# Products of the layer borders and the gated product of the classical FFN tiles kept in PSUM instead of SBUF

## The chip, the cores and the metric

The kernel runs on one core of one Trainium2 chip. The metric is the device time of one execution in microseconds (us), as the median of several executions. Six resources matter here: TensorE (PE, with its weight loads PEld), VectorE (DVE), ScalarE (ACT), GpSimd (POOL), and the DMA queue that SyncE (SP) issues to. TensorE writes its results to PSUM, which has banks of 512 float32 per partition; DVE and ACT read and write PSUM and SBUF, POOL works on SBUF alone.

## What is computed

Two layers of a trunk over 512 latent and 256 context tokens, width 1024. A layer is a half-step SwiGLU FFN, a token mixer (a gated DeltaNet group beside latent attention), and a second half-step FFN. Every sub-layer is wrapped in the same way:

```python
def pre_mod(x, g, m, slot):
    return rmsnorm(x, g) * (1 + m[:, None, 3 * slot + 1]) + m[:, None, 3 * slot]

def post_residual(x, y, g, m, slot, weight):
    return x + weight * m[:, None, 3 * slot + 2] * rmsnorm(y, g)

def ffn_sublayer(x, m, slot, g_pre, g_post, wg, wu, wd):
    h = pre_mod(x, g_pre, m, slot)
    y = (jax.nn.silu(h @ wg) * (h @ wu)) @ wd
    return post_residual(x, y, g_post, m, slot, 0.5)
```

So between any two sub-layers there is a *border*: the sum of squares of y, its norm's factor, the residual, the sum of squares of the new x, that norm's factor, and the modulated input of the next sub-layer.

## The kernel before

**Layout.** Activations lie transposed: eight tiles of 128 features, each with 768 token columns. Columns are worked on in three groups of 256: G_A and G_B (latent) and G_C (context). In what follows a letter behind a stage names its group (z_A, post_B). Every matrix product is made of three float32r products, from a high and a low part of both operands, so each border ends by splitting its result z into `zh` (rounded) and `zl` (the rest).

**The border** is a generator per group. `post` (L414) waits for the sum of squares `ss` of y; `rb1` (L145) reduces it on PE into a PSUM bank of two buffers (`aux`, L137), DVE and POOL make the factors (L158, L159), and `rb2` (L162) has PE broadcast them over all partitions, into columns 0 to 255 of the same bank (R). ACT copies R into SBUF (L425). For each of the eight feature tiles a product y*R goes to a slot `t` (L432: on DVE for five tiles, on POOL for tiles 0, 3 and 5), and DVE adds t times the gate to x (L434). ACT squares the new x, and POOL and DVE in turn add the squares up (L404, L405). `prez` (L448) makes the factors of the next norm by `rb1` and `rb2`, and `z_tile` (L465) works per feature tile: DVE multiplies x, a column and R (read from PSUM) into a slot t (L469), ACT adds the shift and rounds, which gives zh (L472). Towards an FFN (slot 0 or 2), ACT also writes the unrounded z into y (L476), and zl is z minus zh (L477: DVE for even tiles, POOL for odd). Towards the mixer (slot 1) even tiles make zl on DVE straight from t (L479), and odd tiles by ACT in place and POOL (L481, L482).

The slots of `post` and `z_tile` are the same ring: `slot(1)` (L391) hands out three pieces of 256 columns of one SBUF tile in turn, whoever asks.

**The FFN.** Its first three column tiles of hidden features (f = 0, 1, 2) are computed "classically", by `mm3` from zh and zl: f = 0 and 1 group by group while the border still runs, f = 2 afterwards over all columns. `evac` (L541) turns the two banks of a tile, gate `pg` and up `pu`, into the hidden value in pieces of 256 columns: ACT Silu of pg into SBUF `sg` (L546), DVE product of pu and sg into sg (L547), ACT rounds sg into `gh` (L538), DVE writes the rest into `gl` (L539). Banks for matrix products come from a ring of six (`bank`, L131). All other tiles (f = 3 to 21) go by `fast`, a Strassen-like scheme whose operands `combine` (L550) prepares on DVE, ACT and POOL from y right after the border (L560 to L578); its own evacuation (L616 to L619) already keeps the product in its bank.

**What sets the order.** Borders run beside matrix work: `down` (L753) and `mix_out` produce y group by group and call `step()` between products, which advances the generators of the groups before; `mix_pre` (L826) does the same while the next products of the mixer run, and `ffn` while tiles f = 0 and 1 do. `drain(g)` runs a group's generator to its end. This is the program order. Each engine's own queue is then written by the framework's scheduler (`schedule_with_timeline_sim=True`), which goes through the program in order of priority and time; work under `high_priority` comes first. On the chip each queue runs strictly in that order, and an instruction that waits holds up those behind it. Adaptive-norm vectors of later stages are computed by DVE in the background (`pump`, `flush`, L243).

Of the kernel before, what the change touches and what calls it, by code (L numbers as in the profile page):

```python
# [20 lines left out]
EPS = 1e-6  # L21
# [13 lines left out]
class K:  # L35
# [126 lines left out]
    def rb2(self, ps, r, n):  # L162

        for t in range(n // P):
            self.nc.tensor.matmul(ps[:, t * P : (t + 1) * P], r[:, t : t + 1].to_broadcast([P, P]), self.ident, start=True, stop=True)
        return ps[:, :n]

    def rbcast(self, ss, n, inv_d, eps):
        return self.rb2(*self.rb1(ss, n, inv_d, eps))
# [75 lines left out]
    def begin(self):  # L245
# [17 lines left out]

        def factor(g):
            r = self.new_rs()
            nc.scalar.copy(r, self.rbcast(xs[g], g[1], 1.0 / 1024, EPS))
            return r

        m = {part: self.cp.tile([P, KT, 2], F32, name=f"m0_0_{part}") for part in range(2)}
# [35 lines left out]
        for q in range(4):  # L305
# [32 lines left out]
                R = {g: factor(g) for g in (G_A, G_B)}  # L338
            for g in (G_A, G_B):
                for k in (2 * q, 2 * q + 1):  # L340
                    self.z_tile(0, 0, g, R[g], k)
            yield
        load_x(G_C)

# [70 lines left out]
    def post(self, l, slot, g, ss, final=False, nxt=None):  # L415

        nc = self.nc
        off, n, v = g
        for _ in range(1):
            yield  # L420
        rb = self.rb1(ss, n, 1.0 / 1024, EPS)
        for _ in range(1):
            yield
        R = self.new_rs()
        nc.scalar.copy(R, self.rb2(*rb))  # L425
        pg = self.pg[l, slot]
        ss2 = None if final else self.ssx
        first = [True, True]
        for k in range(KT):
            t = self.slot(1)  # L430
            eng = nc.gpsimd if (41 >> k) & 1 else nc.vector
            eng.tensor_tensor(out=t, in0=self.y[k][:, off : off + n], in1=R, op=ALU.mult)  # L432
            xs = self.X[k][:, off : off + n]
            nc.vector.scalar_tensor_tensor(out=xs, in0=t, scalar=pg[:, k, v : v + 1], in1=xs, op0=ALU.mult, op1=ALU.add)  # L434
            if final:
                nc.sync.dma_start(self.out[:, k, off : off + n], xs)
            else:
                i = (178 >> k) & 1
                self.sumsq(ss2[i], xs, first[i], nc.vector if i else nc.gpsimd)
                first[i] = False  # L440
            if k % 3 == 2:
                yield
        if not final:
            for _ in range(3):
                yield
            yield from self.prez(nxt[0], nxt[1], g, ss2)

    def prez(self, l, slot, g, ss):  # L448
        nc = self.nc
        off, n, v = g  # L450
        yield
        rb = self.rb1(ss, n, 1.0 / 1024, EPS)
        for _ in range(1):
            yield
        R = self.rb2(*rb)
        for k in range(KT):
            self.z_tile(l, slot, g, R, k)
        if slot != 1 and (l, slot) != (0, 0):

            if (l, slot) not in self.xsv:  # L460
                self.xsv[l, slot] = self.dram_tile(f"xs{l}{slot}", [KT, P, NT])
            for k in range(KT):
                nc.sync.dma_start(self.xsv[l, slot][k][:, off : off + n], self.X[k][:, off : off + n])

    def z_tile(self, l, slot, g, R, k):  # L465
        nc = self.nc
        off, n, v = g
        t = self.slot(1)
        nc.vector.scalar_tensor_tensor(out=t, in0=self.X[k][:, off : off + n], scalar=self.scol[l, slot][:, k, v : v + 1], in1=R, op0=ALU.mult, op1=ALU.mult)  # L469
        h, lo = self.zh[k][:, off : off + n], self.zl[k][:, off : off + n]  # L470
        b = self.M[l, slot, 0][:, k, v : v + 1]
        nc.scalar.activation(h, t, AF.Identity, bias=b)  # L472
        if slot != 1:

            zf = self.y[k][:, off : off + n]
            nc.scalar.activation(zf, t, AF.Identity, bias=b)  # L476
            (nc.vector if (85 >> k) & 1 else nc.gpsimd).tensor_sub(lo, zf, h.bitcast(F32))  # L477
        elif (85 >> k) & 1:
            nc.vector.scalar_tensor_tensor(out=lo, in0=t, scalar=b, in1=h.bitcast(F32), op0=ALU.add, op1=ALU.subtract)  # L479
        else:  # L480
            nc.scalar.activation(t, t, AF.Identity, bias=b)  # L481
            nc.gpsimd.tensor_sub(lo, t, h.bitcast(F32))  # L482

    def open_w(self):
        self.wp = self.pool("w", side="right")
# [38 lines left out]
    def ffn(self, l, i, slot, groups, post, begin=None):  # L524
# [7 lines left out]
        def loads(f, eng=None):  # L532
            return [self.load_w(d["wu"][l, i, f, u], eng=eng) for u in range(2)]

        def gated(j, h, off, n):
            with self.hp(0):
                o = gh[j][:, off : off + n]
                nc.scalar.copy(o, h)  # L538
                nc.vector.tensor_sub(gl[j][:, off : off + n], h, o.bitcast(F32))  # L539

        def evac(j, pg, pu, off, n):  # L541
            for o in range(0, n, 256):
                sg = self.sg()[:, :256]
                c = slice(o, o + 256)
                with self.tc.high_priority():
                    nc.scalar.activation(sg, pg[:, c], AF.Silu)  # L546
                    nc.vector.tensor_tensor(out=sg, in0=pu[:, c], in1=sg, op=ALU.mult)  # L547
                gated(j, sg, off + o, 256)

        def combine():  # L550

# [282 lines left out]
    def mix_in(self, l, last):  # L834
# [127 lines left out]
        def low_rank(t0, cnt, gain, dst, groups, inv_d):  # L962
# [28 lines left out]
            def scaled():  # L991
              for g in gs:
                off, n, v = g
                R = self.rb2(*rb[g])
                for j in range(cnt):
                    x = st[j][:, off : off + n]
                    nc.vector.scalar_tensor_tensor(out=x, in0=x, scalar=gain[:, j : j + 1], in1=R, op0=ALU.mult, op1=ALU.mult)
# [1018 lines left out]
```

## Time and profile before

| | us |
|---|---|
| median of 3 executions | 3329.84 |
| lowest, highest | 3324.64, 3330.06 |
| the profiled execution's own time | 3321.82 |
| its span, first to last instruction | 3320.0 |
| PE busy | 3058.4 (92%) |
| DVE busy | 2562.9 (77%) |
| ACT busy | 1377.4 (41%) |
| POOL busy | 1345.7 (41%) |

The profile is one execution, recorded by the hardware. Busy is time in which an instruction of the engine ran; an "idle before" is the time an engine sat still before an instruction, with the instruction (engine, tile, line) that ended the wait behind an arrow. A group's mean is over all instructions of one line, engine and operand shape. `ps`, `mixp` and `rb` are PSUM tiles, `bt` the slots, `be` sums of squares and R, `m` the modulation columns.

### The profile page before, as it was taken

To read this page: it belongs to the slowest core of one execution; us is meant where nothing else is said; L and a number is where in the kernel's file an instruction comes from. 1 tells how busy PE (TensorE), PEld (TensorE's weight loads), DVE (VectorE), ACT (ScalarE), POOL (GpSimd) and SP (SyncE) were. 2 spreads that over 40 slices of the span, in tenths; PEclk is the share of its full clock that TensorE was granted. 3 is DMA by queue.
4 is the path that set the end of the run, shared out by engine and by line. 5 is a ranking of instruction groups with operands and counts; after the bars stand their busy time and mean duration, and the time that the engine had idled before them with its cause. 6 is when DMAs were issued, how large, how long until landed. Compare 5 with 4: busy or idle time off the path is not lost. (4 is left out here: it accounts for less than half of the span.)

```text
span 3320.0 us, 53695 instructions
## 1 busy us (share of the span) xinstructions
PE 3058.4 (92%) x20836; PEld 2785.7 (84%) x20836; DVE 2562.9 (77%) x4337; ACT 1377.4 (41%) x2600; POOL 1345.7 (41%) x1060
## 2 busy tenths in 40 slices
PE   7899999889889998999998899999989788989998
PEld 4799989878787798999998798999877676788998
DVE  7888887777778959677777977777677879776777
ACT  4333223544445644322234432223454346544343
POOL 5322122544655765222215511221544546753233
PEclk8999999889999899999999999999989899989999
DMA  6233333222310122323324233332322310224233
GB/s 221 101 122 122 107 127 117 94 73 54 97 64 10 51 86 81 108 91 107 101 73 158 82 109 114 121 127 89 104 98 64 88 46 17 91 90 134 96 106 98
DMA packets 149816, 318.68 MB, mean 96 GB/s; under 512 B 38185, under 2 KB 79529, under 8 KB 149561
## 3 DMA queue, kind: packets, MB, share of 16 engines
q1 hardware_dynamic: 149560, 315.25, 28.9%
q8 instruction: 163, 2.67, 0.3%
q14 instruction: 93, 0.75, 0.1%
HBM read 285.17 MB, written 30.03 MB: 95 GB/s over the span
## 5 line engine op out<-in xcount | busy, mean ns | idle before, releaser
L94 POOL TENSOR_TENSOR wlo<-wraw,whi 128x1024 fp32r<-128x1024 f32 (+1 forms) x228 | 580.3, 2554 | 1357.5 <-ACT whi L93 1304.9
L93 ACT CAST whi<-wraw 128x1024 fp32r<-128x1024 f32 (+2 forms) x482 | 469.5, 978 | 692.0 <-PE ps L776 338.5
L519 PE MATMUL ps<-zh,whi 128*128 128x256 f32 (+1 forms) x1208 | 389.5, 331 | 25.2 <-DVE sg L547 13.3
L608 PE MATMUL ps<-zh,whi 128*128 128x384 f32 (+1 forms) x1216 | 392.2, 323 | 8.0 <-DVE sg L547 4.5
L609 PE MATMUL ps<-zl,whi 128*128 128x384 f32 (+1 forms) x1216 | 392.1, 322 | 2.5 <-DVE zl L586 2.5
L610 PE MATMUL ps<-zh,wlo 128*128 128x384 f32 (+1 forms) x1216 | 390.8, 322 | 0.0
L520 PE MATMUL ps<-zl,whi 128*128 128x256 f32 (+1 forms) x1208 | 382.9, 327 | 5.0 <-DVE zl L477 5.0
L775 PE MATMUL ps<-gh,whi 128*128 128x512 f32 (+1 forms) x1008 | 349.5, 354 | 21.3 <-ACT gh L618 18.9
L776 PE MATMUL ps<-gl,whi 128*128 128x512 f32 (+1 forms) x1008 | 338.3, 352 | 17.3 <-DVE gl L619 17.3
L522 PE MATMUL ps<-zh,wlo 128*128 128x256 f32 (+1 forms) x1208 | 351.1, 324 | 0.0
L94 DVE TENSOR_TENSOR wlo<-wraw,whi 128x1024 fp32r<-128x1024 f32 (+1 forms) x254 | 298.1, 1175 | 31.3 <-ACT whi L93 29.9
L778 PE MATMUL ps<-gh,wlo 128*128 128x512 f32 (+1 forms) x1008 | 293.3, 348 | 0.0
L519 PEld LDWEIGHTS ps<-zh,whi 128*128 128x128 f32 x1208 | 236.8, 199 | 56.8 <-DVE sg L547 14.0
L520 PEld LDWEIGHTS ps<-zl,whi 128*128 128x128 f32 x1208 | 238.3, 198 | 24.5 <-DVE zl L477 6.1
L775 PEld LDWEIGHTS ps<-gh,whi 128*128 128x128 f32 x1008 | 191.7, 192 | 65.2 <-ACT gh L618 21.8
L608 PEld LDWEIGHTS ps<-zh,whi 128*128 128x128 f32 x1216 | 229.4, 189 | 10.9 <-ACT whi L93 4.8
L243 DVE CUSTOM_DVE_ANT_0 abraw<-abraw,srow 128x1024 f32<-128x1024 f32 x128 | 208.0, 1625 | 33.2 <-DMA abraw<-in_wat 31.2
L776 PEld LDWEIGHTS ps<-gl,whi 128*128 128x128 f32 x1008 | 193.5, 192 | 46.7 <-DVE gl L619 19.6
L609 PEld LDWEIGHTS ps<-zl,whi 128*128 128x128 f32 x1216 | 229.5, 189 | 3.5 <-DVE zl L586 3.2
L610 PEld LDWEIGHTS ps<-zh,wlo 128*128 128x128 f32 x1216 | 229.4, 189 | 0.0
L522 PEld LDWEIGHTS ps<-zh,wlo 128*128 128x128 f32 x1208 | 222.4, 199 | 6.5 <-issue 1.0
L243 DVE CUSTOM_DVE_ANT_0 adot<-abraw,srow 128x1024 bf16<-128x1024 f32 x96 | 151.3, 1576 | 63.2 <-DMA abraw<-in_wat 62.8
(394 smaller groups left out, 7722.3 us busy)
## 6 DMA issues: line engine op xcount, KB each, us to landing
wraw<-in_wu SPq DMA_DIRECT2D x176, 512.0 KB, 3.3
abraw<-in_wat SPq DMA_DIRECT2D x128, 512.0 KB, 3.3
wraw<-in_wd SPq DMA_DIRECT2D x88, 512.0 KB, 3.5
wraw<-in_wi SPq DMA_DIRECT2D x44, 512.0 KB, 3.4
wraw<-in_wo SPq DMA_DIRECT2D x16, 512.0 KB, 4.0
xs<-x SPq DMA_DIRECT2D x64, 128.0 KB, 1.7
x<-xs SPq DMA_DIRECT2D x64, 128.0 KB, 3.4
x<-in_x SPq DMA_DIRECT2D x48, 128.0 KB, 3.7
```

Source lines behind the costliest of these rows:

```text
L93: nc.scalar.copy(hi[:, :n], raw[:, :n])
L94: (eng or nc.gpsimd).tensor_sub(lo[:, :n], raw[:, :n], hi[:, :n].bitcast(F32))
L243: self.nc.vector.tensor_tensor_reduce(out=dst, in0=w, in1=self.srow[:, v, a:b], scale=1.0, scalar=start, op0=ALU.mult, op1=ALU.add, accum_ ...
L519: nc.tensor.matmul(ps, wh, self.zh[k][:, off : off + n], start=first, stop=False)
L520: nc.tensor.matmul(ps, wh, self.zl[k][:, off : off + n], start=False, stop=False)
L522: nc.tensor.matmul(ps, wl, self.zh[k][:, off : off + n], start=False, stop=last)
L608: nc.tensor.matmul(ps, w[0][:, c], xh, start=k == 0, stop=False)
L609: nc.tensor.matmul(ps, w[0][:, c], xl, start=False, stop=False)
L610: nc.tensor.matmul(ps, w[1][:, c], xh, start=False, stop=k == 3)
L775: nc.tensor.matmul(ps, wh[:, o : o + P], gh[j][:, off : off + n], start=j == 0, stop=False)
L776: nc.tensor.matmul(ps, wh[:, o : o + P], gl[j][:, off : off + n], start=False, stop=False)
L778: nc.tensor.matmul(ps, wl[:, o : o + P], gh[j][:, off : off + n], start=False, stop=j == nf - 1)
```

## The change

Four edits, all in PSUM banks that are there already.

- `rb2` returns the whole bank. `post` reads R where it stands, without ACT's copy, and puts its products into columns 256 and on of that bank. All eight products run on DVE.
- `z_tile` puts t of even tiles into that half of the bank; odd tiles keep an SBUF slot.
- zl of even tiles is always made by DVE from t, the shift and zh. Towards an FFN this takes the place of the subtraction from y; y is still written by ACT.
- `evac` of the classical tiles writes pu times Silu back into pu; ACT and DVE make gh and gl from there.

```diff
--- before.py
+++ after.py
@@ -163,7 +163,7 @@
 
         for t in range(n // P):
             self.nc.tensor.matmul(ps[:, t * P : (t + 1) * P], r[:, t : t + 1].to_broadcast([P, P]), self.ident, start=True, stop=True)
-        return ps[:, :n]
+        return ps
 
     def rbcast(self, ss, n, inv_d, eps):
         return self.rb2(*self.rb1(ss, n, inv_d, eps))
@@ -263,7 +263,7 @@
 
         def factor(g):
             r = self.new_rs()
-            nc.scalar.copy(r, self.rbcast(xs[g], g[1], 1.0 / 1024, EPS))
+            nc.scalar.copy(r, self.rbcast(xs[g], g[1], 1.0 / 1024, EPS)[:, :256])
             return r
 
         m = {part: self.cp.tile([P, KT, 2], F32, name=f"m0_0_{part}") for part in range(2)}
@@ -338,7 +338,7 @@
                 R = {g: factor(g) for g in (G_A, G_B)}
             for g in (G_A, G_B):
                 for k in (2 * q, 2 * q + 1):
-                    self.z_tile(0, 0, g, R[g], k)
+                    self.z_tile(0, 0, g, R[g], k, pt)
             yield
         load_x(G_C)
 
@@ -421,15 +421,14 @@
         rb = self.rb1(ss, n, 1.0 / 1024, EPS)
         for _ in range(1):
             yield
-        R = self.new_rs()
-        nc.scalar.copy(R, self.rb2(*rb))
+
+        ps = self.rb2(*rb)
+        R, t = ps[:, :n], ps[:, 256 : 256 + n]
         pg = self.pg[l, slot]
         ss2 = None if final else self.ssx
         first = [True, True]
         for k in range(KT):
-            t = self.slot(1)
-            eng = nc.gpsimd if (41 >> k) & 1 else nc.vector
-            eng.tensor_tensor(out=t, in0=self.y[k][:, off : off + n], in1=R, op=ALU.mult)
+            nc.vector.tensor_tensor(out=t, in0=self.y[k][:, off : off + n], in1=R, op=ALU.mult)
             xs = self.X[k][:, off : off + n]
             nc.vector.scalar_tensor_tensor(out=xs, in0=t, scalar=pg[:, k, v : v + 1], in1=xs, op0=ALU.mult, op1=ALU.add)
             if final:
@@ -452,9 +451,9 @@
         rb = self.rb1(ss, n, 1.0 / 1024, EPS)
         for _ in range(1):
             yield
-        R = self.rb2(*rb)
+        ps = self.rb2(*rb)
         for k in range(KT):
-            self.z_tile(l, slot, g, R, k)
+            self.z_tile(l, slot, g, ps[:, :n], k, ps)
         if slot != 1 and (l, slot) != (0, 0):
 
             if (l, slot) not in self.xsv:
@@ -462,24 +461,25 @@
             for k in range(KT):
                 nc.sync.dma_start(self.xsv[l, slot][k][:, off : off + n], self.X[k][:, off : off + n])
 
-    def z_tile(self, l, slot, g, R, k):
+    def z_tile(self, l, slot, g, R, k, ps):
+
+
         nc = self.nc
         off, n, v = g
-        t = self.slot(1)
+        even = k % 2 == 0
+        t = ps[:, 256 : 256 + n] if even else self.slot(1)
         nc.vector.scalar_tensor_tensor(out=t, in0=self.X[k][:, off : off + n], scalar=self.scol[l, slot][:, k, v : v + 1], in1=R, op0=ALU.mult, op1=ALU.mult)
         h, lo = self.zh[k][:, off : off + n], self.zl[k][:, off : off + n]
         b = self.M[l, slot, 0][:, k, v : v + 1]
         nc.scalar.activation(h, t, AF.Identity, bias=b)
-        if slot != 1:
-
-            zf = self.y[k][:, off : off + n]
+
+        zf = t if slot == 1 else self.y[k][:, off : off + n]
+        if slot != 1 or not even:
             nc.scalar.activation(zf, t, AF.Identity, bias=b)
-            (nc.vector if (85 >> k) & 1 else nc.gpsimd).tensor_sub(lo, zf, h.bitcast(F32))
-        elif (85 >> k) & 1:
+        if even:
             nc.vector.scalar_tensor_tensor(out=lo, in0=t, scalar=b, in1=h.bitcast(F32), op0=ALU.add, op1=ALU.subtract)
         else:
-            nc.scalar.activation(t, t, AF.Identity, bias=b)
-            nc.gpsimd.tensor_sub(lo, t, h.bitcast(F32))
+            nc.gpsimd.tensor_sub(lo, zf, h.bitcast(F32))
 
     def open_w(self):
         self.wp = self.pool("w", side="right")
@@ -532,20 +532,16 @@
         def loads(f, eng=None):
             return [self.load_w(d["wu"][l, i, f, u], eng=eng) for u in range(2)]
 
-        def gated(j, h, off, n):
-            with self.hp(0):
-                o = gh[j][:, off : off + n]
-                nc.scalar.copy(o, h)
-                nc.vector.tensor_sub(gl[j][:, off : off + n], h, o.bitcast(F32))
-
         def evac(j, pg, pu, off, n):
+
             for o in range(0, n, 256):
                 sg = self.sg()[:, :256]
-                c = slice(o, o + 256)
+                c, d = slice(o, o + 256), slice(off + o, off + o + 256)
                 with self.tc.high_priority():
                     nc.scalar.activation(sg, pg[:, c], AF.Silu)
-                    nc.vector.tensor_tensor(out=sg, in0=pu[:, c], in1=sg, op=ALU.mult)
-                gated(j, sg, off + o, 256)
+                    nc.vector.tensor_tensor(out=pu[:, c], in0=pu[:, c], in1=sg, op=ALU.mult)
+                nc.scalar.copy(gh[j][:, d], pu[:, c])
+                nc.vector.tensor_sub(gl[j][:, d], pu[:, c], gh[j][:, d].bitcast(F32))
 
         def combine():
 
@@ -991,7 +987,7 @@
             def scaled():
               for g in gs:
                 off, n, v = g
-                R = self.rb2(*rb[g])
+                R = self.rb2(*rb[g])[:, :n]
                 for j in range(cnt):
                     x = st[j][:, off : off + n]
                     nc.vector.scalar_tensor_tensor(out=x, in0=x, scalar=gain[:, j : j + 1], in1=R, op0=ALU.mult, op1=ALU.mult)
```

## Rows read from the trace of the kernel before

**Rows 1.** The profile's page, busy time and share of the span by engine

```profile
PE 3058.4 (92%) x20836; PEld 2785.7 (84%) x20836; DVE 2562.9 (77%) x4337; ACT 1377.4 (41%) x2600; POOL 1345.7 (41%) x1060
```

**Rows 2.** Busy time by stretch; us, PE, PEld, DVE, ACT, POOL busy, granted clock, DMA

```profile
625.00:634.50 9.50, 5.14 (x23) 4.41 (x21) 4.51 (x12) 3.65 (x10) 5.72 (x8) 0.72 0.00 0
...
646.70:655.00 8.30, 3.51 (x16) 2.93 (x15) 4.42 (x11) 1.99 (x5) 1.51 (x3) 0.68 0.47 182
```

**Rows 3.** PE's waits; total us, times, longest us

```profile
PE rb L155 <- POOL be L405: 22.9, 8, 6.3
...
PE rb L155 <- DVE be L405: 15.0, 9, 4.9
...
PE ps L519 <- DVE sg L547: 13.3, 3, 6.6
...
PE ps L608 <- DVE sg L547: 4.5, 2, 2.4
```

**Rows 4.** Groups by line and shape; busy us, mean ns, idle before

```profile
L432 DVE TENSOR_TENSOR bt<-y,be 128x256 f32<-128x256 f32 x80 | 53.2, 679 | 7.7 <-ACT be L425 7.5
...
L434 DVE SCALAR_TENSOR_TENSOR x<-bt,m,x 128x256 f32<-128x256 f32 x128 | 74.1, 607 | 0.3
...
L469 DVE SCALAR_TENSOR_TENSOR bt<-x,m,rb 128x256 f32<-128x256 f32 x120 | 53.8, 476 | 17.3 <-PE rb L165 12.9 <-POOL zl L482 3.5 <-ACT y L476 0.3
...
L809 DVE TENSOR_TENSOR y<-y,ps 128x256 f32<-128x256 f32 x88 | 35.7, 415 | 27.0 <-PE ps L806 27.0
...
L477 DVE TENSOR_TENSOR zl<-y,zh 128x256 fp32r<-128x256 f32 x44 | 26.6, 604 | 6.9 <-ACT y L476 6.9
...
L539 DVE TENSOR_TENSOR gl<-sg,gh 128x256 fp32r<-128x256 f32 x33 | 23.8, 742 | 1.8 <-ACT gh L538 1.8
...
L472 ACT ACTIVATE zh<-bt,m 128x256 fp32r<-128x256 f32 x136 | 66.6, 501 | 69.6 <-DVE bt L469 69.1
...
L432 POOL TENSOR_TENSOR bt<-y,be 128x256 f32<-128x256 f32 x48 | 47.8, 1001 | 37.8 <-DVE x L434 27.5 <-ACT be L425 10.0
```

**Rows 5.** Two of these lines, least, median and greatest ns

```profile
L434 DVE SCALAR_TENSOR_TENSOR x<-bt,m,x x128: 470/474/964, 594.3 to 3316.7; 128x256 f32<-128x256 f32 x128
...
L469 DVE SCALAR_TENSOR_TENSOR bt<-x,m,rb x120: 466/476/485, 71.5 to 2968.3; 128x256 f32<-128x256 f32 x120
```

**Rows 6.** Groups of ACT, what ended its idle time

```profile
L404 ACT ACTIVATE bt<-ps 128x256 f32<-128x256 f32 x35 | 12.9, 383 | 36.1 <-DVE y L1791 21.1 <-DVE be L405 7.7 <-POOL be L405 7.3
...
L1524 ACT COPY kp<-kps 64x512 f32<-64x512 f32 x8 | 4.7, 583 | 4.1 <-DVE g L1523 4.0
```

**Rows 7.** Timeline of a border into the mixer, DVE and PE

```profile
610.78 1.26 DVE L469 SCALAR_TENSOR_TENSOR bt<-x,m,rb 128x256 f32<-128x256 f32 x3
...
618.21 0.85 DVE L432 TENSOR_TENSOR bt<-y,be 128x256 f32<-128x256 f32 x1
...
627.98 0.43 DVE L405 TENSOR_TENSOR be<-be,bt 128x256 f32<-128x256 f32 x1 [0.48 <-ACT bt L404]
...
629.04 1.72 PE L155 MATMUL rb<-ones,be 128*128 128x1 f32 x8 [3.77 <-POOL be L405]
...
633.46 1.26 DVE L469 SCALAR_TENSOR_TENSOR bt<-x,m,rb 128x256 f32<-128x256 f32 x3 [0.90 <-PE rb L165]
...
649.61 1.80 PE L155 MATMUL rb<-ones,be 128*128 128x1 f32 x8 [2.64 <-POOL be L405]
```

**Rows 8.** Timeline of an FFN's start after combine, PE and DVE

```profile
1313.85 0.58 PE L519 MATMUL ps<-zh,whi 128*128 128x256 f32 x1 [6.56 <-DVE sg L547]
...
1313.72 1.98 DVE L94 TENSOR_TENSOR wlo<-wraw,whi 128x512 fp32r<-128x512 f32 x1
...
1315.95 1.71 DVE L539 TENSOR_TENSOR gl<-sg,gh 128x256 fp32r<-128x256 f32 x1
```

**Rows 9.** Timeline of the end, ACT and DVE

```profile
3310.39 0.37 ACT L425 COPY be<-rb 128x256 f32<-128x256 f32 x1 [4.52 <-PE rb L165]
...
3316.32 0.87 DVE L434 SCALAR_TENSOR_TENSOR x<-bt,m,x 128x256 f32<-128x256 f32 x2
```

## The prediction, on record before the changed kernel was run

> **What bounds the kernel now.** I read the page first: PE is busy 92% of the span, DVE 77% [rows 1]. A shorter instruction on DVE, ACT or POOL is therefore worth only what PE gets back, and PE's waits say where that can be. At the borders PE waits at `rb1` for a sum of squares, 17 times and 37.9 us in total (22.9 for POOL's last addition, 15.0 for DVE's), and at the start of an FFN for the bank of a gated product, five times and 17.8 us [rows 3]. Nearly all that this change can win lies in the first figure; the second is what it can make worse. The stretches show the picture: in 9.50 us of a border into the mixer PE was busy 5.14, in another 8.30 us only 3.51, at a granted clock of 0.72 and 0.68 [rows 2]. (I leave the clock out of the sum; a shorter idle would at most add to a gain.)
>
> The timeline of that border says why PE waits [rows 7]. z_C begins on DVE at 610.78. The residual of G_A begins only at 618.21, where z_C ends, because both take their t from one ring of three slots. Its last addition ends at 628.41, PE's rb1 starts at 629.04 after a wait of 3.77, z_A follows at 633.46, and the same again for G_B up to the rb1 at 649.61, after a wait of 2.64. The stages stand in a row although they belong to different groups.
>
> **The durations.** DVE's adds to x take 474 ns in the median but up to 964; the product with R read from PSUM takes 466 to 485, always [rows 5]. All that DVE does at 256 columns from two SBUF tensors is drawn out: y*R 679 ns in the mean, the add to x 607, zl 604, gl 742, while a form with one operand in PSUM takes 415 or 476 [rows 4]. The long ones are those that POOL works beside (the third of its products takes 1001 ns). With t, R or pu in PSUM I take 0.415 for a product or subtraction and 0.476 for the three-operand form. Three of the latter take 1.26 [rows 7], so one follows another after 0.39, and with the same overlap of 0.08 a product after 0.34.
>
> **The change, part by part.**
>
> *Residual, on the DVE queue.* Per group DVE did five products and eight adds, 5 x 0.679 + 8 x 0.607 = 8.3 us, POOL three products of 1.0 and ACT a copy of 0.37 [rows 4, 9]. Now DVE does 8 x 0.34 + 8 x 0.39 = 5.8. No slot of the ring is used, so the residual of the next group need not wait for z: it can fill DVE's gaps there, if the scheduler queues it so. For the border of [rows 7]: z_C is 12 instructions at 0.39 (4.7 us), post_A 5.8, its additions 3 x 0.34 = 1.0, about 1.0 of gaps that stay, and 1.3 for the last square on ACT and the last addition. That puts G_A's sum at 610.8 + 13.8 = 624.6, 4.4 us earlier than the rb1 of 629.04. Only the wait of 3.77 can be won. For G_B the same 13.8 stands against 649.61 - 633.46 = 16.15: 2.3 of its wait of 2.64. So 6.1 per border, and two such borders: **-12.2**. The ends are 0 (queues ordered as now) and -14 (every wait of the kind: 2 x (3.77 + 2.64) = 12.8, and something for the copies on ACT).
>
> *The other borders.* Of the 37.9 us about 25 remain [rows 3]. There DVE also has background dot products and zh/zl of an FFN to do, and is its own limit; the slots matter less. What is left is the shorter work, about 2.5 us per group of 256, on roughly three groups whose rb1 PE waits for, with part of it hidden: **-6**, ends 0 and -12.
>
> *z tiles.* The new wait is here. R and t now share a bank, and ACT reads t in it. Two rows show what the framework does with that: ACT squares a PSUM tile that nobody changes, yet waited 21.1 us for DVE's copy of the same tile; and a copy of partitions 64 to 127 of a bank waited 4.0 us for a DVE instruction that reads partitions 0 to 63 [rows 6]. Accesses of two engines to one bank are put in order, reads too. So after every even tile DVE may not read R for the next (odd) tile before ACT has finished zh, 0.50 us [rows 4]; behind it wait the even zl, the next products and whatever stands in DVE's queue. Towards the mixer a pair of tiles then takes 0.48 + 0.50 + about 0.1 + 2 x 0.39 = 1.9 us, against (618.21 - 610.78)/4 = 1.86 now [rows 7]: nothing lost, and the wait is what post_A fills. Towards an FFN ACT reads t twice (zh, then y), so the pair takes 2.3, or 2.7 where the queue puts y ahead of the next zh: 1.6 to 3.2 us more for a group. This counts where `combine` follows and needs the last y, at four FFN starts. DVE has other subtractions to do there, so I take **+4**, 1.0 each; ends 0 and +13. In return even zl falls from 0.604 to 0.476, and zl no longer waits for y (that wait was 6.9 us in total).
>
> The Trainium skill (PSUM — Partial Sum Buffer, "PSUM bank collisions raise a hardware error") says that two engines must never be in one bank and partition quadrant at once, reads against reads included, and that software has to keep them apart by bank. The two waits of [rows 6] agree with it. By the rule the sum is as it stands; if disjoint columns ran freely, the +4 would go.
>
> *Gated product.* The bank of pu used to come free after DVE's product; now ACT's rounding and DVE's gl must have read it. At 1313.85 PE had waited 6.56 for such a bank, and in today's order gl stands behind a DVE instruction of 1.98 us at 1313.72 and ends only at 1317.66; with gl at 0.41 the bank would come at 1316.4, 2.6 later [rows 8]. Five waits of this kind: two of that length, the others with less queued in between, say 1.0 to 1.5. Together +8, less some 3 for gl itself (742 to 415 ns on 33 instructions, half of them where DVE is full): **+5**, ends -4 and +15.
>
> *End and start.* In the last residual nothing hides anything. The copy at 3310.39 goes, and the 16 instructions of DVE end at 3310.4 + 5.9 = 3316.3 instead of 3317.19; G_A's residual, queued before, is shorter by about 1.0: **-2**. The first z tiles wait for DMA and the dot products; I cost them at 0, ends -1 and +3.
>
> POOL loses 48 us and ACT 6 [rows 4, 9]; both are 41% busy, and nothing waits for what they gain. No DMA changes. Each residual holds one of two `aux` buffers longer, but the next rb1 that needs it waits for that residual's sum anyway.
>
> **Sum:** -12.2 - 6 + 4 + 5 - 2 = **-11 us**: a span of 3309, and 3311 for the profiled execution of 3321.82. That one lies 8.0 below the median of 3329.84 and below all three shown. Put on the median: **3319**, 0.33% faster. A measurement of this kernel can tell about 0.2%, 6.7 us, from no change.
>
> **Rivals.**
>
> *Nothing measurable.* The scheduler leaves the residual behind z, where it is now, or other work fills DVE. Then only durations count: 2 x 3 us at the mixer borders, -3 at the others, +9 for z and pu, -2: -2, so 3328. For it: the scheduler orders by simulated time, and DVE is 77% busy. Against it: z leaves gaps that only the slots kept empty.
>
> *Slower: the bank of pu.* Each FFN start waits for a chain DVE, ACT, DVE instead of one product. If gl stands behind the subtractions of `combine`, or a wait grows by 6 us instead of 1 to 2.6, five waits cost 30 instead of 8. With the rest as above: -11 + 22 = +11, 3341. It decides as soon as a wait grows by over 3.8 in the mean (19 us in all). For it: these waits are already as long as 6.6 us, and gl has no high priority. Against it: gl in PSUM is short, and program order puts it early.
>
> *No ordering by bank.* DVE reads R while ACT reads t: z is faster than now, -15, 3315. [Rows 6] speak against it.
>
> **How the numbers follow.** The forecast has 0.55, nothing measurable 0.23, slower 0.17, no ordering 0.05. Nearly all of the forecast's and the last's chance lies below 3323.2: faster 0.59. Slower by over 6.7 us 0.15, with part of the slow rival just short of it; same 0.26. The range runs from 3303 (-14, -12 and -2 with no loss at z or pu, near -27) to 3337, which takes in all of the second case and the lower half of the third.
>
> **What would show it.** Right: in the border into the mixer, residual adds to x between z's products, rb1 at about 625 on today's scale, no waits of 3.8 and 2.6 there; the add to x at 476 ns for all 128; the total for rb1 down from 37.9 to about 20. z: DVE idle before products of odd tiles, released by ACT's zh. pu: PE released by gl, waits of 17.8 us grown to some 25. Wrong: residual products that still begin where z ends; pu waits above 35 us; or a total of rb1 waits that has fallen while the span has not.

## The result, and the profile after

The changed kernel takes 3348.38 us (median of 4) against 3329.46 for the kernel before on the same chip: a ratio of 1.0061, interval 1.0044 to 1.0079. It is 0.6% slower where 0.33% faster was forecast, and it lies above the range. The profiled execution took 3347.06 us; its span is 3345.3, which is 25.3 longer than before.

The page's first part of the changed kernel, as [rows 1]:

```profile
PE 3073.6 (92%) x20836; PEld 2796.2 (84%) x20836; DVE 2524.6 (75%) x4385; ACT 1368.4 (41%) x2582; POOL 1293.7 (39%) x1012
```

DVE lost 38 us of work, POOL 52 and ACT 9 (the text had 48 for POOL and 6 for ACT). PE got nothing of it. Its 20836 matmuls took 15.2 us longer than before, at a mean granted clock of 0.947 instead of 0.953 of full speed, and it sat idle for 271.7 us instead of 261.6 (the span less the busy time). So of the 25.3 us, 15.2 are slower matmuls and only 10.1 are idle time. The groups by line and shape of the changed kernel (busy us, mean ns, idle before) answer to [rows 4]:

```profile
L433 DVE SCALAR_TENSOR_TENSOR x<-rb,m,x 128x256 f32<-128x256 f32 x128 | 61.4, 480 | 1.8
...
L431 DVE TENSOR_TENSOR rb<-y,rb 128x256 f32<-128x256 f32 x128 | 54.5, 425 | 9.6 <-PE rb L165 7.4
...
L480 DVE SCALAR_TENSOR_TENSOR zl<-rb,m,zh 128x256 fp32r<-128x256 f32 x60 | 28.8, 479 | 8.0 <-ACT zh L474 4.3 <-ACT y L478 3.4
...
L544 DVE TENSOR_TENSOR gl<-ps,gh 128x256 fp32r<-128x256 f32 x33 | 13.4, 417 | 1.6 <-ACT gh L543 0.9
```

Every single instruction became as short as predicted: the add to x 480 ns (607 before), the product 425 (679), even zl 479 (604), gl 417 (742). So the durations were right, and the loss is one of order, of waits and of PE's slower matmuls. PE's waits (total us, times, longest us) answer to [rows 3]:

```profile
PE ps L519 <- ACT sg L541: 12.7, 3, 5.7
...
PE rb L155 <- DVE rba L158: 9.0, 6, 3.6
PE rb L155 <- DVE be L405: 8.9, 5, 2.1
PE ps L519 <- ACT bt L404: 8.5, 1, 8.5
PE rb L155 <- POOL be L405: 8.0, 1, 8.0
PE ps L520 <- DVE zl L480: 7.4, 3, 5.4
...
PE ps L604 <- ACT sg L541: 5.3, 5, 1.8
```

The waits of rb1 fell from 37.9 to 25.9 (the forecast said about 20). The waits at an FFN's start for the banks of a gated product are 18.0 from ACT's Silu, and 2.4 from gl in two rows not shown, against 17.8: they grew by 2.6 in all, and the Silu, not gl, releases most of them. Two others stand out: 8.5 for a square of y in the mixer's output product (1.8 before), and 9.0 (none before) for `rba`, DVE's first step of a norm's factors.

The border into the mixer is the timeline to lay beside [rows 7]; the first fence row is z_C's first tile, the second post_A's first product (start, duration, engine, line):

```profile
618.03 0.49 DVE L471 SCALAR_TENSOR_TENSOR rb<-x,m,rb 128x256 f32<-128x256 f32 x1 [0.90 <-PE rb L165]
619.21 0.43 DVE L431 TENSOR_TENSOR rb<-y,rb 128x256 f32<-128x256 f32 x1 [0.70 <-PE rb L165]
...
615.95 0.98 PE L155 MATMUL rb<-ones,be 128*128 128x1 f32 x4 [2.42 <-DVE rba L158]
632.23 1.22 PE L155 MATMUL rb<-ones,be 128*128 128x1 f32 x8
633.81 0.58 PE L155 MATMUL rb<-ones,be 128*128 128x1 f32 x4 [0.37 <-DVE rba L158]
```

Here the forecast holds: post_A starts 1.2 us behind z_C, not 7.4, and rb1 comes 14.2 after z_C began (18.3 before, 13.8 forecast), with no wait in front. But z_C itself starts 7.25 us later than before. The stage gave 4 us back to a delay that came from the stage ahead of it. Laid side by side matmul by matmul, the two traces differ most where the mixer's output product hands over to the second FFN: some +17 us in layer 0 and +7.5 in layer 1. The stretch in layer 0, from the same matmul to the same matmul, before and after, in the form of [rows 2]:

```profile
1211.80:1358.10 146.30, 134.97 (x1001) 130.06 (x1001) 119.56 (x203) 70.53 (x150) 77.11 (x62) 0.98 0.27 91
1214.60:1377.50 162.90, 141.00 (x1002) 133.22 (x1003) 118.41 (x212) 69.67 (x147) 65.05 (x53) 0.93 0.25 81
```

It is 16.6 us longer: 10.6 of it are idle time of PE, and 6.0 are matmuls that took longer at a granted clock of 0.93 instead of 0.98 (1 is 2.4 GHz; the lower of the two levels, 0.5, is 1.2 GHz). In these traces more idle time and a lower clock go together; no run changes the clock by itself.

### The profile page after: what moved, and what is told of

It reads as the page before. It is cut to its first block, busy times and chain, and to the rows that moved or that the text cites. A ratio compares the mean times of both kernels' runs of the same rounds, so it can differ in the third digit from the quotient of the medians.

```text
span 3345.3 us, 53671 instructions
## 1 busy us (share of the span) xinstructions
PE 3073.6 (92%) x20836; PEld 2796.2 (84%) x20836; DVE 2524.6 (75%) x4385; ACT 1368.4 (41%) x2582; POOL 1293.7 (39%) x1012
## 5 line engine op out<-in xcount | busy, mean ns | idle before, releaser
L519 PE MATMUL ps<-zh,whi 128*128 128x256 f32 (+1 forms) x1208 | 375.3, 335 | 32.5 <-ACT sg L541 12.7
L520 PE MATMUL ps<-zl,whi 128*128 128x256 f32 (+1 forms) x1208 | 383.0, 331 | 10.1 <-DVE zl L480 7.4
L604 PEld LDWEIGHTS ps<-zh,whi 128*128 128x128 f32 x1216 | 229.6, 189 | 10.1 <-ACT sg L541 8.2
L604 PE MATMUL ps<-t42h,whi 128*128 128x384 f32 (+1 forms) x608 | 195.3, 321 | 2.2 <-DVE gl L615 2.2
```

Of the source, the lines that this page charges most:

```text
L519: nc.tensor.matmul(ps, wh, self.zh[k][:, off : off + n], start=first, stop=False)
L520: nc.tensor.matmul(ps, wh, self.zl[k][:, off : off + n], start=False, stop=False)
L604: nc.tensor.matmul(ps, w[0][:, c], xh, start=k == 0, stop=False)
```

## The experiments

All ratios are against the kernel before on the same chip, with 95% intervals; 0.1% is 3.3 us.

**One part at a time.** Four kernels: the residual's edit alone, the z tiles' alone, the gated product's alone, and the change without its z tiles. Each is the diff of the front section with the other hunks left out.

> The kernel before with the residual's edit alone (R and t in PSUM, all products on DVE, no copy of R); z tiles and gated product as before. By the sum of the prediction -12.2 - 6 - 2 = -20: about 3309. Theory z (the loss of 19 us comes from z's even tiles in the bank of R, whose trips between DVE and ACT string out everything queued beside them): 3309 to 3320, faster. Theory residual (DVE's chain of products through one t, with squares of x in front of the squares of y that free mix_out's banks, is itself the loss): 3340 or more, with a PE wait of several us behind an ACT square of a product tile.

> The kernel before with the z tiles' edit alone (even tiles in the other half of the bank of R, zl of even tiles by DVE from there); residual and gated product as before. By the sum of the prediction +4: 3333. Theory z: most of the 19 us, 3341 to 3348. Theory residual: 3325 to 3335.

> The kernel before with the edit of the gated product alone (product kept in the bank of pu). By the sum of the prediction +5: 3334. Theories z and residual: no more than that, 3327 to 3334. Theory pu (the rival of the prediction: the bank is free too late): 3341 or more, waits of PE at the first products of a tile grown to over 30 us in total.

> The changed kernel with the old z tiles (residual and gated product as changed). By the sum of the prediction -20 + 5 = -15: 3314. Theory z: 3314 to 3325, faster than before by over 0.2%. Theory residual: 3345, as the changed kernel. If no single edit carries the loss and effects do not add (theory order: any edit makes the scheduler write other queues, and background dot products land in other places), this run and the three others need not add up: the sum of the three single differences would miss the 19 us of the whole by over 10.

Measured: residual alone 3325.34 (0.9997, 0.9988 to 1.0006); z tiles alone 3355.34 (1.0084, 1.0071 to 1.0098); gated product alone 3327.85 (1.0010, 1.0002 to 1.0019); all but z 3328.66 (1.0007, 0.9998 to 1.0016); kernel before 3325.4. The z tiles carry the loss: +28 us by the ratio (30 by the medians), where the sum had +4. The gated product's +3 agrees with its +5, and the rival that made its bank decide has fallen. The residual shows neither the forecast gain of 20 nor a loss. The three single differences give 30 us, the whole 20: with the new residual, z costs 18 instead of 28. Why it costs less there was not tried.

**What in z.** DVE's waits ahead of even zl, in the kernel with the z tiles alone:

```profile
DVE zl L481 <- ACT zh L475: 15.2, 24, 1.6
DVE zl L481 <- ACT y L479: 13.3, 15, 1.6
```

These are 28.5 us, where the kernel before has 6.9 and, for the mixer's form, 1.8. zl needs zh, so the first row alone would prove little. It does not need y, and yet 13.3 us of waits end with y, where with t in slots (the kernel without the bank, below) none does: two reads of one bank are put in order.

That 28.5 is close to the loss is chance, because these are waits of DVE. In the same trace PE sits idle 10.6 us more than in the kernel before (272.2 against 261.6), and its matmuls take 17.7 us longer (3076.1 against 3058.4), at a granted clock of 0.946 instead of 0.953. What happens to the tiles shows in the tiles ahead of the second FFN. ACT's timeline before:

```profile
1291.77 0.49 ACT L472 ACTIVATE zh<-bt,m 128x256 fp32r<-128x256 f32 x1
1292.17 0.49 ACT L476 ACTIVATE y<-bt,m 128x256 f32<-128x256 f32 x1
1292.57 0.49 ACT L472 ACTIVATE zh<-bt,m 128x256 fp32r<-128x256 f32 x1
...
1293.37 0.49 ACT L472 ACTIVATE zh<-bt,m 128x256 fp32r<-128x256 f32 x1
```

and the same tiles with the z edit alone, ACT and then DVE:

```profile
1296.78 0.47 ACT L475 ACTIVATE zh<-rb,m 128x256 fp32r<-128x256 f32 x1 [4.99 <-DVE rb L472]
1297.15 0.47 ACT L479 ACTIVATE y<-rb,m 128x256 f32<-128x256 f32 x1
1298.56 0.51 ACT L475 ACTIVATE zh<-bt,m 128x256 fp32r<-128x256 f32 x1 [0.94 <-DVE bt L472]
...
1299.42 0.48 ACT L475 ACTIVATE zh<-rb,m 128x256 fp32r<-128x256 f32 x1
...
1296.26 0.49 DVE L472 SCALAR_TENSOR_TENSOR rb<-x,m,rb 128x256 f32<-128x256 f32 x1 [1.99 <-PE rb L165]
1297.65 0.48 DVE L481 SCALAR_TENSOR_TENSOR zl<-rb,m,zh 128x256 fp32r<-128x256 f32 x1 [0.91 <-ACT y L479]
1298.05 0.47 DVE L472 SCALAR_TENSOR_TENSOR bt<-x,m,rb 128x256 f32<-128x256 f32 x1
1298.44 0.55 DVE L561 TENSOR_TENSOR y<-y 128x384 f32<-128x384 f32 x1
1298.91 0.48 DVE L472 SCALAR_TENSOR_TENSOR rb<-x,m,rb 128x256 f32<-128x256 f32 x1
```

Before, ACT is the limit here and never idle: 1.60 us for two tiles (1291.77 to 1293.37). Now DVE stands until ACT has done both its reads of t (0.91), then zl, then the odd product, and ACT stands in its turn (0.94): 2.64 us for two tiles (1296.78 to 1299.42), and 3.13 for the next two (to 1302.55). The wait stands ahead of zl, where the text had it ahead of the odd product. Four kernels take this apart.

```diff
 # z_rsb, in prez                          # z_stt, in z_tile
-ps = self.rb2(*rb)                        -t = ps[:, 256 : 256 + n] if even else self.slot(1)
+ps = self.rb2(*rb); R = self.new_rs()     +t = self.slot(1)
+nc.scalar.copy(R, ps[:, :n])              # z_mix: even, in t and in zl, becomes
 # z_tile reads R from SBUF                #   even and slot == 1; else as before
 # z_yfirst, towards an FFN, even tiles (z_rsb_y: with the copy of R as well)
+nc.scalar.activation(zf, t, AF.Identity, bias=b)     # into y
+nc.scalar.copy(h, zf); nc.vector.tensor_sub(lo, zf, h.bitcast(F32))
```

> The z tiles' edit without its bank: all tiles' t in the ring of SBUF slots as before, even zl by the three-operand form from t. Theory bank (R and t in one bank): no loss, 3320 to 3332. Theory form (0.48 to 0.60 us from SBUF in place of 0.42 to 0.60): 3335 or more.

> As the run with the z tiles' edit alone, but ACT first copies R out of the bank into SBUF (0.37 us per group), so the bank holds only the even tile's t in use, and the product of the next odd tile touches no bank that ACT reads. Theory R (the loss of 30 us of that run is DVE kept from reading R while ACT reads t twice): most of it goes, 3325 to 3334. Theory zl (the loss is the even zl, which must wait for ACT's second read of t, or its longer form): still 3345 or more.

> The z tiles' edit only at the borders into the mixer, where ACT reads an even t once; towards an FFN, where it reads it twice, as before. The prediction took a loss of 0 here: 3325. By the trace of the run with all z tiles changed, 2 to 6 of its 30 us come at the two borders into the mixer: 3327 to 3332. If the loss were in each pair of tiles alike, it would be some 40% of 30 us: 3337.

> The z tiles' edit alone, but towards an FFN ACT reads an even t once: it writes z into y, and zh and zl of that tile are then made from y in SBUF. Theory bank (what costs is how long ACT keeps DVE out of the bank that holds both R and t): the loss of 30 us falls to 15 or less, 3331 to 3341. Theory pair (any trip from DVE to ACT and back in one bank costs the same, however long): 3345 or more.

> Both: R copied to SBUF and ACT reading an even t once towards an FFN. So DVE and ACT meet in the bank only where the result of one is the input of the other. Theory bank: the loss of 11.5 us of the run with R in SBUF falls to 5 or less, 3326 to 3332. If the remaining 11.5 us were the copy of R (0.37 us on ACT ahead of each z) or t's single buffer: 3336 or more.

Measured: without the bank 3327.3 (1.0007, 0.9997 to 1.0016), so the form of zl costs nothing that can be told, and the bank costs nearly all. R out of the bank 3338.58 (1.0040, 1.0028 to 1.0053): half of the loss goes. Only towards the mixer 3331.38 (1.0015, 1.0007 to 1.0024): 5 us, not 0, and the rest falls to the borders towards an FFN. One read by ACT 3341.56 (1.0051, 1.0039 to 1.0063): 11 of the 28 us go, a little less than expected. Both together 3350.06 (1.0076, 1.0063 to 1.0088), where 5 us or less were expected: a miss. PE's waits show what is left. First R out of the bank alone, then both:

```profile
PE ps L523 <- DVE zl L483: 23.7, 20, 5.4
...
PE ps L522 <- ACT zh L477: 18.3, 16, 4.2
```

```profile
PE ps L528 <- ACT zh L480: 18.6, 7, 4.8
PE ps L529 <- DVE zl L481: 16.5, 10, 5.8
```

(With the z tiles alone the two kinds are 8.0 and 7.0.) L480 and L481 serve even tiles only. Odd products, freed from the bank, run ahead of the even ones, while every even tile must take its turn through the one t, and PE wants the tiles in order. So by these rows what is left lies with t itself. ACT's copy of R ahead of each group (0.37 us, which both kernels have) was not tried apart from it, and why both together are worse than either is not settled. The next kernel gives the even tiles the two halves of the bank in turn:

```diff
-t = ps[:, 256 : 256 + n] if even else self.slot(1)
+t = ps[:, k % 4 * 128 : k % 4 * 128 + n] if even else self.slot(1)
```

> As the run with R copied to SBUF, and the even tiles' t take the two halves of the bank in turn, so that one may be written while ACT reads the other. If what was left there (11.5 to 13 us) is that all even tiles share one t: 3333 or less. If the two engines are kept apart by the bank, not by the columns: 3337 to 3341, no change.

Measured 3337.42 (1.0042, 1.0029 to 1.0055): no change, and PE's waits for even tiles stay as they were:

```profile
PE ps L523 <- DVE zl L483: 23.2, 20, 5.4
...
PE ps L522 <- ACT zh L477: 18.4, 16, 4.2
```

None of the 60 even products starts ahead of the zl of the even tile before it, though their columns differ. With slots they do: at 610.78 in the kernel before, three products run in a row ahead of the first zl ([rows 7]). So different columns do not free them; that leaves the bank, which is one tile to the framework, so that the two cannot be told apart here. Whether another program order of the same accesses would help was not tried. The Trainium skill (PSUM — Partial Sum Buffer, "PSUM bank collisions raise a hardware error") has it so: software guards PSUM by bank and quadrant (a quarter of the partitions), or simply by bank, not by address, and disjoint columns don't excuse two engines. The run agrees on the columns (1.0042 with two halves, 1.0040 with one). The second wait of [rows 6], which the prediction lays beside that page, goes further than the rule: partitions 64 to 127 and 0 to 63 are different quadrants, which the rule lets pass.

**Where the residual's gain went.** The new residual gains at the mixer and loses elsewhere, by the traces. Its split, with `new` put on six of the sixteen residuals: four beside the mixer's first products (G_A and G_B, in both layers) and the last two, G_A and G_B at the end of the kernel.

```diff
+new = final or slot == 0 and g != G_C        # post_mix; post_rest: not (...)
+t = ps[:, 256 : 256 + n] if new else self.slot(1)   # else R, t and POOL's products as before
```

> The residual's edit only for the four residuals of G_A and G_B that run beside the mixer's first products (two per layer), and for the last residual of the kernel. z tiles and gated product as before. By the prediction's terms for these (-12.2 and -2): 3313. By the trace of the run with the residual's edit everywhere (z_C to rb1 14.3 us instead of 18.3, z_A to rb1 14.3 instead of 16.15, so 3.9 + 1.85 per layer, and 2 at the end): -13.5, 3313. Rival (the time that the stage gains is lost at once to the products behind it): 3323 to 3327.

> The complement of that: the residual's edit everywhere but in those four and the last. The prediction took -6 for them: 3320. Theory pace (beside down and mix_out the single t makes DVE take the tiles one by one, each behind an addition to y that waits for PE's product, and the squares of x on ACT hold up those of y): +8 to +13, 3334 to 3339. If it is neutral, 3325 to 3328, then the gain at the mixer was not one either.

Measured: 3311.8 (0.9957, 0.9945 to 0.9970) and 3338.65 (1.0041, 1.0029 to 1.0053). So -14.3 and +13.6 us, and they cancel, as the residual alone has it (0.9997). The border of [rows 7] in the first of them, PE's rb1:

```profile
626.16 0.38 PE L155 MATMUL rb<-ones,be 128*128 128x1 f32 x2
626.85 0.83 PE L155 MATMUL rb<-ones,be 128*128 128x1 f32 x6 [0.30 <-DVE be L405]
628.05 0.58 PE L155 MATMUL rb<-ones,be 128*128 128x1 f32 x4 [0.37 <-DVE rba L158]
```

rb1 at 626.16 instead of 629.04, its wait 0.3 instead of 3.77. In the other kernel the residual that runs beside `down` (its first product, and the first, fifth and last addition):

```profile
593.03 0.43 DVE L437 TENSOR_TENSOR rb<-y,rb 128x256 f32<-128x256 f32 x1 [0.26 <-PE rb L165]
593.50 0.48 DVE L439 SCALAR_TENSOR_TENSOR x<-rb,m,x 128x256 f32<-128x256 f32 x1
...
598.60 0.48 DVE L439 SCALAR_TENSOR_TENSOR x<-rb,m,x 128x256 f32<-128x256 f32 x1
...
606.19 0.48 DVE L439 SCALAR_TENSOR_TENSOR x<-rb,m,x 128x256 f32<-128x256 f32 x1
```

13.6 us from first product to last addition, 9.0 before (593.04 to 602.0). Beside the mixer's output product it is 23.3 instead of 13.8. Product and addition go strictly in turn through one t, tile by tile, with whatever the queue holds in between. Is it the one t, or POOL's three products, now on DVE?

```diff
 # post_rest_slot: R read from the bank     # post_rest_dve: R copied to SBUF as before
-t = ps[:, 256 : 256 + n] if new ...        -t = ps[:, 256 : 256 + n] if new ...
+t = self.slot(1)                           +t = self.slot(1)
```

> As the run with the residual's edit everywhere but beside the mixer's first products and at the end (which cost 12 us), but t goes to the ring of three SBUF slots as before; DVE still makes all eight products and reads R from the bank. Theory one t (product and addition strictly in turn through one piece of PSUM set the pace): the 12 us go, 3322 to 3330. Theory DVE (the three products that POOL made are what is too much for DVE here): 3334 to 3341.

> The same without any PSUM: R copied to SBUF by ACT and t in slots, as before; only POOL's three products are moved to DVE in those residuals. Theory one t: no loss, 3322 to 3330 (or 2 to 4 us more for the longer forms from SBUF). Theory DVE: 3334 or more.

Measured: 3320.98 (0.9984, 0.9973 to 0.9995) and 3332.67 (1.0025, 1.0013 to 1.0037). It is the one t: back in three slots, with R still in PSUM, a loss of 13.6 becomes a gain of 5.3. Both theories missed part of it: without PSUM the three products on DVE do cost, 8 us. The products' rows in the better kernel, R from the bank and R from SBUF:

```profile
L437 DVE TENSOR_TENSOR bt<-y,rb 128x256 f32<-128x256 f32 x80 | 29.7, 411 | 3.4 <-PE rb L165 3.4
L437 DVE TENSOR_TENSOR bt<-y,be 128x256 f32<-128x256 f32 x30 | 20.0, 681 | 3.5 <-ACT be L430 3.3
```

and its residual beside `down` begins:

```profile
592.67 1.08 DVE L437 TENSOR_TENSOR bt<-y,rb 128x256 f32<-128x256 f32 x3 [0.26 <-PE rb L165]
593.67 0.87 DVE L439 SCALAR_TENSOR_TENSOR x<-bt,m,x 128x256 f32<-128x256 f32 x2
...
599.36 1.36 DVE L439 SCALAR_TENSOR_TENSOR x<-bt,m,x 128x256 f32<-128x256 f32 x2
```

8.1 us to the end, with three products in one piece.

**A wait that went for nothing.** In the mixer's output product of the changed kernel, PE waits 8.49 us, and ACT's queue says for what:

```profile
1267.00 0.58 PE L519 MATMUL ps<-zh,whi 128*128 128x256 f32 x1 [8.49 <-ACT bt L404]
...
1264.35 0.42 ACT L404 ACTIVATE bt<-x 128x256 f32<-128x256 f32 x1 [4.93 <-DVE x L433]
1265.65 0.42 ACT L404 ACTIVATE bt<-x 128x256 f32<-128x256 f32 x1 [0.89 <-DVE x L433]
1266.56 0.38 ACT L404 ACTIVATE bt<-ps 128x256 f32<-128x256 f32 x1 [0.49 <-DVE be L405]
```

The square of y that must still read the bank stands behind squares of an x that DVE's drawn-out residual delivers late. The residual alone has the same wait (7.38). Read from y instead, the square needs no bank:

```diff
-self.sumsq(ss, ps, q == 0, ...)
+self.sumsq(ss, yv, q == 0, ...)
```

> The kernel with the residual's edit alone, and the squares of y in the mixer's output product read from y in SBUF instead of the product's bank, so that DVE's copy alone frees the bank. Theory squares (the gain of the residual at the mixer borders is given back where PE waits 7.4 us for a bank that ACT's squares of y must still read, behind squares of the new x): the wait goes and 5 to 8 us with it, 3317 to 3320. Theory DVE (the residual's products would hold the stage up anyway, by the sums that rb1 waits for): 3323 to 3327, the wait moved to rb1 or to DVE's copy of the product.

Measured 3324.87 (0.9992, 0.9982 to 1.0001): the wait is gone, and no more than 1 or 2 us with it, within what can be told. A residual that is late by itself, as the one t makes it, fits that: the wait only showed where.

**Together.**

```diff
 # post_mix_evac: post_mix with the gated product's hunk; _hp: gh and gl under high_priority too
 # best: post_mix_evac, with R read from the bank and t in slots in all other residuals
```

> The kernel with the residual's edit only beside the mixer's first products and at the end, and the gated product's edit as in the change. If the parts add (the gated product alone cost 0.10%, 3 us): 3311.8 + 3 = 3315. If the gated product's cost was an accident of one order of the queues: 3308 to 3312.

> The same, with the rounding into gh and the product's rest gl under high priority too, so that they no longer stand behind other work in their queues and the bank of pu comes free sooner. If PE's waits for that bank are what the edit costs: 3 us or more below the run without, 3309 to 3312. If they are not: within 2 us of it.

> The change without its z tiles, and with t of the residual in the slots again everywhere but in the four residuals beside the mixer's first products and the last one; R is read from the bank in all of them. If the parts add: -0.43% (those five residuals), -0.16% (R in the bank, t in slots elsewhere), 0 (gated product): 0.6% faster, about 3304. If the second part's gain lies in the same waits as the first's: 0.43%, 3310.

Measured: 3310.73 (0.9955, 0.9943 to 0.9967), 3309.17 (0.9959, 0.9947 to 0.9972), 3309.05 (0.9964, 0.9950 to 0.9977). On top of the good half of the residual the gated product costs nothing, high priority changes nothing, and the slots' 0.16% does not add. These three and the kernel with the good half alone cannot be told apart; all beat the kernel before by about 0.4%, the changed one by 1%.

## Why the prediction was wrong

**z tiles (+4): the step that failed first.** The mechanism stood in the text: reads of two engines in one bank are put in order, the pair becomes 2.3 or 2.7. Its size was off in three places. The pair "now" was taken from the border into the mixer (1.86), where the pair ahead of an FFN takes 1.60; it became 2.64 and more, so a group loses 4 to 6 us there (4 pairs by 1.04 to 1.53), not 1.6 to 3.2. It was charged at four FFN starts with 1.0 each, where 11 groups pass towards an FFN, nine of them with R and t in one bank, and PE was late behind several. And towards the mixer "nothing lost" was 5 us. Measured 28 alone and about 18 beside the other edits; the upper end was 13.

**Clock: a term put at nothing.** The text left the granted clock out, because a shorter idle would "at most add to a gain". The idle time grew instead, and the clock added to the loss: slower matmuls make up 15.2 of the 25.3 us, at 0.947 instead of 0.953, and 17.7 of 28.3 with the z tiles alone.

**Residual at the mixer (-12.2) and at the end (-2):** together -14.2 forecast, -14.3 measured; that the two meet so closely is luck. The border is as worked out (z_C to rb1 14.2 to 14.5, forecast 13.8). In the trace of the kernel with these six residuals alone, the same matmuls at the mixer's border take 110.2 us instead of 118.6 in layer 0 and 113.2 instead of 121.3 in layer 1. PE's idle time falls by 6.4 in each, where the text has 6.1; the rest, 2.1 and 1.7, is shorter matmuls, at 0.92 instead of 0.89 and 0.93 instead of 0.90. At the end, PE's last wait for a sum is 1.70 instead of 4.42 us. But from PE's last broadcast to the last addition the changed kernel takes 8.55 us, 1.3 more than before, since the eight pairs take 0.98 each, as below, and not 0.73: 1.4 won, of 2. Small losses between these places, 3 to 4 us, bring the sum back to 14.3.

**Other borders (-6): the step that failed next.** It counted DVE's time and not the order of the work. The "0.34 and 0.39" for product and addition hold for instructions that don't wait for each other; and in a full queue one t lets only one tile be under way. Measured +13.6. With t in slots the same edit gives -5.3, which is the -6 of the text: R in PSUM was the gain, t in PSUM the loss. The `aux` buffer that each residual holds longer was costed at nothing. With t in slots, where R holds it to the last product, PE's waits for `rba` are 0.7 us, so holding it costs little by itself. With t in it they are 8.4 (9.0 in the changed kernel); whether the buffer or the late residual makes them is not shown.

**Gated product (+5):** 3.3 alone (0.7 to 6.3), nothing measurable on top of the better residual. gl was short, as the text had against its rival, and PE's waits for it are 2.4 us. The 3 us that the text takes off for gl do not follow from its numbers: half of 33 times 0.327 is 5.4, which would have made the term +2.6.

**The rivals.** "Nothing measurable" gave 3328, which fits the change without z (3328.66) by a sum of gains and losses that it did not foresee. The slower rival had the right side and the wrong place: its price sits in z's bank, not in pu's. "No ordering by bank" is refuted: 13.3 us of DVE's waits ahead of zl end with a read by ACT that zl does not need.

The text named as a sign of error "a total of rb1 waits that has fallen while the span has not". That is what came: the waits fell from 37.9 to 25.9, and the span is 25.3 longer.

## What to carry to other kernels

PSUM as scratch pays where one engine alone works in the bank: R read by DVE, or product and addition beside other DVE work that fills the gaps. As soon as a second engine reads a piece of the bank, count each of its reads as time in which the first may use no column of it, at every place where the code runs, with the pair's time taken from that place. A wait of TensorE can cost more than its own length: in these traces a border with 6.4 us less idle time became 8 us shorter, and a stretch with 10.6 more became 16.6 longer. And a shorter instruction is no gain where it costs the second buffer: t in three slots was worth 19 us more than t in one half of a bank.

## What the runs showed of the hardware

Two dependent DVE instructions don't overlap. The last residual of the changed kernel, where DVE has nothing else:

```profile
3340.53 0.43 DVE L431 TENSOR_TENSOR rb<-y,rb 128x256 f32<-128x256 f32 x1
3341.00 0.48 DVE L433 SCALAR_TENSOR_TENSOR x<-rb,m,x 128x256 f32<-128x256 f32 x1
...
3341.52 0.43 DVE L431 TENSOR_TENSOR rb<-y,rb 128x256 f32<-128x256 f32 x1
```

Product to addition 0.47, addition to the next product 0.52: 0.99 per tile, each starting some 0.04 after the one before has ended. Independent ones follow after 0.39 (three in 1.26, [rows 7]) and 0.34 (three in 1.08, above), before the one ahead has ended. So the chain costs 0.25 per tile more than the sum of the forecast, 2 us per group. The Trainium skill (VectorE: DVE Perf Modes, "The DRAIN you can't avoid") says that chaining without semaphores saves nothing over a semaphore after each instruction. That is a measurement of copies, and no run here tries it. What this trace adds is that a product and an addition that depend on each other take a third more than two that don't (0.99 against 0.73).
